# Up projection of the second feed-forward by Strassen's scheme, with the sums of products on VectorE

## The chip, the cores and the metric

The kernel runs on one core of a Trainium2 chip. The metric is the device time of one execution, in microseconds (us); less is better. In the profile PE is TensorE (the matrix engine), PEld its weight loads, DVE VectorE, ACT ScalarE, POOL GpSimd, SP the engine that only issues DMAs.

## What is computed

The reference is one step of a two-layer trunk on 512 latent and 128 context tokens of width 1024. Each layer is a mixer and a gated feed-forward; the change lies in the feed-forward of the second layer:

```python
def conv_ffn(h, w_up, w_conv, w_down):
    a, g = jnp.split(h @ w_up, 2, axis=-1)
    return (jax.nn.gelu(dwconv3(a, w_conv)) * g) @ w_down

xs = xs + gt_s2 * conv_ffn(rmsnorm(xs, g_ffn[l]) * (1.0 + sc_s2) + sh_s2, w_up[l], w_conv_ffn[l], w_down[l])
```

`h` is 640 x 1024, `w_up` 1024 x 5632 (2816 features `a` and 2816 gates `g`), `w_down` 2816 x 1024. `dwconv3` is a convolution of width 3 along the tokens, feature by feature; the context tokens are a sequence of their own. A final RMSNorm follows.

## The kernel before

Features lie on the 128 partitions, the 640 tokens in the free dimension, in two halves of 320 (`HT`); the second half holds 192 latent and 128 context tokens. The 1024 inputs are 8 blocks k of 128, the 2816 features 22 tiles f of 128 (`NF`). Products are in fp32r. So that they are exact enough, each operand is split into a high part (fp32r, cast on ScalarE) and a low part (the rest, a subtraction on VectorE): `XH`, `XL` for the normed tokens, `wh`, `wl` for weights (`split_w`, L94 to L99), `G[:, 0]`, `G[:, 1]` for the hidden layer. A product is the sum of three matmuls, high by high, high by low and low by high, each 128 x 128 by 128 x 320. A tile of 128 outputs and all tokens thus takes 8 x 3 x 2 = 48 matmuls (`mm_k`, L118), where two neighbours, the halves of the tokens, use the same weights.

`ffn` (L373) runs the tiles in the order a_0, g_0, a_1, g_1, ... through `linear` (L125), which loads a tile of weights (512 KB, tag `raw`, four buffers), splits it (tags `wh` and `wl`, three each) and multiplies. Behind an a tile, `conv3` (L348) takes the convolution out of PSUM, once on ScalarE (L350) and four times on VectorE (L353), then comes gelu on ScalarE (L388, tile `ge`). Behind a g tile, VectorE multiplies by the gelu (L398, tile `pr`), ScalarE casts (L400), VectorE subtracts (L401): `G[f]`. The down projection is done in three groups of features (`GROUPS`: 8, 7 and 7), each as soon as its features are there, eight tiles of outputs in a group; `residual` (L328) adds each into `x` with the layer's gate, three VectorE rows. In the last group the last three tiles go half by half (`tail=3`, `mm_half`), so that the final norm of the first half of the tokens (`final_steps`, `rms_steps`, tile `rbfin`) runs while the second is multiplied.

The norm before the feed-forward (`norm_steps`, `norm_part`, L297) runs between the last matmuls of the attention's output projection (`pop`). For each block k VectorE writes the scaled tokens into a small tile `nt`, ScalarE adds the shift and writes `XH`, VectorE subtracts for `XL` (L307). The first three up tiles run half by half with k outermost, so that TensorE can start on the first blocks; their low parts are taken on GpSimd.

A scheduler sets the order on each engine when the program is built; each engine then runs its own list in order, with semaphores between them. PSUM has eight banks of 512 numbers; here three tiles of two banks and two of one (`use_psum(3, 2)`).

## Time and profile before

| | |
|---|---|
| median of three runs | 1732.78 us (1732.56 to 1733.68) |
| span of the profiled execution | 1733.2 us |
| TensorE busy | 1676.1 us, 97% |
| VectorE busy | 1052.3 us, 61% |
| ScalarE busy | 672.4 us, 39% |
| second feed-forward | from about 1250 us to the end |

The profiled execution is given by its span, from the first to the last instruction; it is 0.4 us above the median of the runs. Busy shares are means over stages with different limits. A TensorE row is shown longer than its share of the time, since matmuls overlap: the pace is read from starts.

### The profile page before, as it was taken

The page shows a single profiled execution, that of the slowest core. Times are in us where ns is not written, and L with a number is a line of the kernel's source. Part 1 is how long each engine was busy: PE and PEld are TensorE (multiplying, and loading weights), DVE is VectorE, ACT ScalarE, POOL GpSimd, SP SyncE. Part 2 cuts the span into 40 slices and gives each one's busy share as a digit, 9 for nine tenths or more (in the row PEclk, how much of TensorE's full clock was granted, in tenths as well). Part 3 has the DMA queues.
Part 4 walks back from the last instruction along what each step waited for, and adds up shares of the span by engine and source line. Part 5 has one row for each costly group of instructions (what it writes and reads, how often), then busy time and mean ns, then how long its engine had stood idle before and what let it go on. Part 6 is the DMA issues. An engine that isn't in the chain of part 4 may idle for free. (4 is left out here: it accounts for less than half of the span.)

```text
span 1733.2 us, 28191 instructions
## 1 busy us (share of the span) xinstructions
PE 1676.1 (97%) x11434; PEld 1596.5 (92%) x11434; DVE 1052.3 (61%) x2089; ACT 672.4 (39%) x1235; POOL 142.2 (8%) x150
## 2 busy tenths in 40 slices
PE   5999999999999999999997999999999999999997
PEld 2699889899999999999997888998999999999997
DVE  5886656666987677777376555555564433433444
ACT  6323346754432133223245565555343312321332
POOL 3110001101000000000023212120100000000001
PEclk9999999999999999999999999999999999999998
DMA  8334422141454454453213111211222222222211
GB/s 325 117 132 163 160 72 71 48 142 59 140 176 147 146 153 144 154 170 104 79 64 101 60 60 47 65 42 52 74 73 74 73 74 73 71 76 85 69 54 61
DMA packets 57121, 175.62 MB, mean 101 GB/s; under 512 B 7632, under 2 KB 15104, under 8 KB 56736
## 3 DMA queue, kind: packets, MB, share of 16 engines
q1 hardware_dynamic: 56800, 173.66, 31.1%
q8 instruction: 90, 1.47, 0.4%
...
q0 software_dynamic: 192, 0.17, 0.0%
HBM read 169.61 MB, written 4.20 MB: 100 GB/s over the span
## 5 line engine op out<-in xcount | busy, mean ns | idle before, releaser
L331 DVE SCALAR_TENSOR_TENSOR x<-pd,mod,x 128x320 f32<-128x320 f32 (+2 forms) x144 | 55.1, 434 | 146.7 <-PE pd L122 137.3
L247 DVE CUSTOM_DVE_ANT_0 adj<-adw,cb 128x1024 f32<-128x1024 f32 x112 | 136.7, 1221 | 1.6
L398 DVE TENSOR_TENSOR pr<-pu,ge 128x384 f32<-128x384 f32 x84 | 37.4, 486 | 108.4 <-PE pu L122 107.6
L353 DVE SCALAR_TENSOR_TENSOR fcb<-pu,cwf,fcb 128x384 f32<-128x384 f32 (+1 forms) x176 | 95.8, 549 | 4.1
L388 ACT ACTIVATE ge<-fcb 128x641 f32<-128x641 f32 x44 | 32.6, 742 | 105.4 <-DVE fcb L353 105.4
L306 ACT ACTIVATE XH<-nt,mod 128x192 fp32r<-128x192 f32 (+1 forms) x96 | 39.6, 466 | 44.0 <-DVE nt L302 43.8
L1120 DVE CUSTOM_DVE_ANT_0 s<-pS,bm 128x384 f32<-128x384 f32 x64 | 34.5, 553 | 30.1 <-PE pS L1119 29.0
L307 DVE SCALAR_TENSOR_TENSOR XL<-nt,mod,XH 128x192 fp32r<-128x192 f32 (+1 forms) x96 | 46.4, 521 | 5.0 <-ACT XH L306 4.9
L1021 DVE TENSOR_SCALAR s<-s,nm 128x384 f32<-128x384 f32 (+1 forms) x80 | 46.3, 586 | 1.8
L1019 ACT ACTIVATE s<-s,nm 128x384 f32<-128x384 f32 x64 | 39.2, 612 | 20.3 <-DVE nm L1120 18.3
L350 ACT ACTIVATE fcb<-pu,cwf 128x384 f32<-128x384 f32 x88 | 46.3, 528 | 1.3
L1194 POOL TENSOR_TENSOR fo<-fo,rs 128x320 f32<-128x320 f32 x8 | 6.9, 888 | 469.8 <-ACT rs L1186 469.8
L1134 ACT COPY pTs<-pS 128x384 f32<-128x384 f32 (+1 forms) x80 | 33.7, 434 | 23.4 <-PE pS L1132 22.7
L1132 PE MATMUL pS<-ident,s 128*128 128x128 f32 x208 | 36.3, 281 | 5.8 <-DVE s L1021 5.8
L98 POOL TENSOR_TENSOR qk00l<-qk,qk00h 128x1024 fp32r<-128x1024 f32 x1 | 2.8, 2761 | 461.6 <-DVE rn L288 461.6
L273 ACT ACTIVATE sqn<-x 128x320 f32<-128x320 f32 x56 | 25.3, 466 | 39.4 <-DVE x L331 35.3
L1094 POOL TENSOR_TENSOR bm<-amask,wr 128x768 f32<-128x768 f32 x16 | 30.7, 1918 | 112.6 <-issue 83.9
L302 DVE SCALAR_TENSOR_TENSOR nt<-x,coefA,rbn 128x192 f32<-128x192 f32 (+1 forms) x96 | 36.7, 430 | 3.6 <-PE rbn L294 3.5
L1112 PE MATMUL pS<-k,q 128*128 128x256 f32 x128 | 31.0, 328 | 7.6 <-DVE k L1047 7.1
L400 ACT CAST G<-pr 128x640 fp32r<-128x640 f32 x44 | 31.8, 728 | 13.4 <-DVE pr L398 13.4
L331 DVE SCALAR_TENSOR_TENSOR x<-pop,mod,x 128x320 f32<-128x320 f32 (+2 forms) x36 | 14.4, 433 | 36.7 <-PE pop L122 26.0
L401 DVE TENSOR_TENSOR G<-pr,G 128x640 fp32r<-128x640 f32 x44 | 36.0, 819 | 0.0
...
## 6 DMA issues: line engine op xcount, KB each, us to landing
u<-in_w_up SPq DMA_DIRECT2D x88, 512.0 KB, 3.5
adw<-in_w_adaT SPq DMA_DIRECT2D x56, 512.0 KB, 4.1
wa<-in_w_ada SPq DMA_DIRECT2D x40, 512.0 KB, 5.0
...
qk<-in_w_qkv SPq DMA_DIRECT2D x24, 512.0 KB, 3.5
d<-in_w_down SPq DMA_DIRECT2D x16, 512.0 KB, 3.5
qk<-in_w_ab SPq DMA_DIRECT2D x8, 512.0 KB, 3.5
op<-in_w_oab SPq DMA_DIRECT2D x6, 512.0 KB, 3.4
```

The costliest lines, as they stand in the source:

```text
L247: dve.tensor_tensor_reduce(out=jk, in0=w, in1=cb[:, s], op0=ALU.mult, op1=ALU.add, scale=1.0, scalar=0.0, accum_out=acc[:, k, s : s + 1])
L302: dve.scalar_tensor_tensor(out=t, in0=x[:, k, c0:c1], scalar=coefA[:, n, k, s : s + 1], in1=rb[:, c0 - a * HT : c1 - a * HT], op0=ALU.mult ...
L306: act.activation(out=oh, in_=t, func=AF.Identity, bias=b)
L307: last = dve.scalar_tensor_tensor(out=ol, in0=t, scalar=b, in1=oh.bitcast(F32), op0=ALU.add, op1=ALU.subtract)
L331: r = dve.scalar_tensor_tensor(out=x[:, k, c0:c1], in0=pt[:, h, c0 - h * HT : c1 - h * HT], scalar=mod[:, l, ch, k, s : s + 1], in1=x[:, k ...
L350: act.activation(out=o, in_=i, func=AF.Copy, scale=w[1])
L353: dve.scalar_tensor_tensor(out=o, in0=i, scalar=w[j], in1=o, op0=ALU.mult, op1=ALU.add)
L398: dve.tensor_tensor(out=o, in0=i_, in1=c, op=ALU.mult)
L401: here[0] = dve.tensor_tensor(out=g[:, 1], in0=pr, in1=g[:, 0].bitcast(F32), op=ALU.subtract).ins
L1019: act.activation(out=s, in_=src, func=AF.Exp, scale=-1.0, bias=nm, accum_out=sm)
L1021: dve.tensor_scalar(out=s, in0=s, scalar1=sm, scalar2=None, op0=ALU.mult)
L1132: pe.transpose(pS[:, j * P : (j + 1) * P], s[:, j * P : (j + 1) * P], ident)
```

## The change

The weights of feature tile f are seen as two by two half blocks: a11 and a12 are the a tile's weights for the inputs k = 0 to 3 and 4 to 7, a21 and a22 the g tile's. The tokens are two by two as well: B11 (k 0 to 3, first half of the tokens), B21 (k 4 to 7, first half), B12 and B22 for the second half. The eight half products of a feature are replaced by seven (Strassen's scheme in Winograd's form), from the fourth feature tile on (`NC = 3`), on 19 of 22. With s = a21 + a22 and t = s - a11 the products are: w1 = a11 with B11, w2 = a12 with B21, w3 = a12 - t with B22, w4 = a22 with T4, w5 = s with T1, w6 = t with T2, w7 = a11 - a21 with T3. T1 to T4 are sums of the token blocks, made once (`sums`), T1 in the place of B12. The norm now keeps its scaled tokens in four tiles `keep`, ScalarE adds the shift to them in place (`shift`, 24 rows), VectorE adds and splits them, eight rows of 1280 elements.

Each product is 4 x 3 = 12 matmuls into one bank (`product`). Three banks hold the sums of a feature, partly accumulated by TensorE (A: w1, then w2; B: w6, then w7, then w4; C: w5, then w3), and read in between by ScalarE (`s1`) and VectorE (`u2`, `u3`, `gg`); the convolution then reads SBUF (`av`, tile `fca`). w4 and w3 of a feature come after w1 and w6 of the next. PSUM is eight tiles of one bank from there on. The down projection is done in four groups (6, 6, 5 and 5 features) instead of three. Other lines of the diff move pools, leave out comments, or set `fo` to six buffers.

```diff
+    def ffn_open(es, l):
+        fc = es.enter_context(tc.tile_pool(name=f"fc{l}", bufs=1, reuse_waits="tile"))
+        fp = es.enter_context(tc.tile_pool(name=f"fp{l}", bufs=2, reuse_waits="tile"))
+        def gtile(nm):
+            return fp.tile([P, 2, T], F32R, tag="G", name=nm, bufs=7)
+        keep = [gtile(f"keep{l}{i}").bitcast(F32).rearrange("p a b -> p (a b)").rearrange("p (k c) -> p k c", k=4)
+                for i in range(4)]
+        return fc, fp, gtile, keep
...
+        B11, B21 = ((XH[:, k : k + 4, 0:HT], XL[:, k : k + 4, 0:HT]) for k in (0, 4))
+        T1, B22 = ((XH[:, k : k + 4, HT:T], XL[:, k : k + 4, HT:T]) for k in (0, 4))
+        T2, T3, T4 = ((TT[:, i, 0], TT[:, i, 1]) for i in range(3))
...
+        def split_t(dst, src):
+            act.copy(out=dst[0], in_=src)
+            dve.tensor_tensor(out=dst[1], in0=src, in1=dst[0].bitcast(F32), op=ALU.subtract)
+        def shift(i):
+            a = i // 2
+            for k in range(4):
+                for c0, c1, s in RANGES[a]:
+                    t = keep[i][:, k, c0 - a * HT : c1 - a * HT]
+                    act.activation(out=t, in_=t, func=AF.Identity, bias=mod[:, l, 3, 4 * (i % 2) + k, s : s + 1])
+        def sums():
+            n11, n21, n12, n22 = keep
+            tt = lambda o, a, b, op: dve.tensor_tensor(out=o, in0=a, in1=b, op=op)
+            yield
+            yield
+            shift(2)
+            shift(3)
+            tt(n22, n22, n12, ALU.subtract)
+            split_t(T3, n22)
+            shift(0)
+            yield
+            tt(n12, n12, n11, ALU.subtract)
+            tt(n11, n22, n11, ALU.add)
+            split_t(T2, n11)
+            shift(1)
+            yield
+            tt(n21, n21, n11, ALU.subtract)
+            split_t(T4, n21)
+            yield
+            split_t(T1, n12)
+            yield
+        NC = 3
+        st = sums()
+        linear([I["w_up"][l, i // 2, i % 2] for i in range(2 * NC)], done_up, f"u{l}_", head=3, spare=True,
+               filler=lambda: next(st, 0))
+        use_psum(0, 8)
+        half = [None, 0]
+        def split_half(src, nm):
+            if half[1] == 0:
+                half[0] = [wp.tile([P, 1024], F32R, tag=t, name=f"{nm}{t}") for t in ("wh", "wl")]
+            h, lo = (w[:, 512 * half[1] : 512 * half[1] + 512] for w in half[0])
+            half[1] ^= 1
+            act.copy(out=h, in_=src)
+            dve.tensor_tensor(out=lo, in0=src, in1=h.bitcast(F32), op=ALU.subtract)
+            return h.rearrange("p (k c) -> p k c", c=P), lo.rearrange("p (k c) -> p k c", c=P)
+        def product(pt, w, b, first, last):
+            o = pt[:, :HT]
+            for k in range(4):
+                for n, (ww, xx) in enumerate(((w[0], b[0]), (w[0], b[1]), (w[1], b[0]))):
+                    pe.matmul(o, ww[:, k], xx[:, k], start=(first and k == 0 and n == 0),
+                              stop=(last and k == 3 and n == 2), skip_group_check=not first)
+        def up(f):
+            tt = lambda o, a, b, op: dve.tensor_tensor(out=o, in0=a, in1=b, op=op)
+            ra, rg = (wp.tile([P, 1024], F32, tag="raw", name=f"u{l}_{f}{q}", bufs=4) for q in "ag")
+            sp.dma_start(out=ra, in_=I["w_up"][l, f, 0])
+            sp.dma_start(out=rg, in_=I["w_up"][l, f, 1])
+            a11, a12, a21, a22 = ra[:, 0:512], ra[:, 512:], rg[:, 0:512], rg[:, 512:]
+            A = pst(f"A{l}_{f}")
+            product(A, split_half(a11, f"w1{f}"), B11, True, True)
+            s1 = fp.tile([P, HT], F32, tag="s1", name=f"s1{l}_{f}")
+            act.copy(out=s1, in_=A[:, :HT])
+            yield
+            ss = fp.tile([P, 2, 512], F32, tag="ss", name=f"ss{l}_{f}", bufs=1)
+            tt(ss[:, 0], a21, a22, ALU.add)
+            tt(ss[:, 1], ss[:, 0], a11, ALU.subtract)
+            B = pst(f"B{l}_{f}")
+            product(B, split_half(ss[:, 1], f"w6{f}"), T2, True, True)
+            u2 = fp.tile([P, HT], F32, tag="u2", name=f"u2{l}_{f}")
+            tt(u2, B[:, :HT], s1, ALU.add)
+            yield
+            product(A, split_half(a12, f"w2{f}"), B21, False, True)
+            av = cin.next()
+            act.copy(out=av[:, 1 : HT + 1], in_=A[:, :HT])
+            tt(a12, a12, ss[:, 1], ALU.subtract)
+            yield
+            tt(a21, a11, a21, ALU.subtract)
+            product(B, split_half(a21, f"w7{f}"), T3, False, True)
+            u3 = fp.tile([P, HT], F32, tag="u3", name=f"u3{l}_{f}", bufs=1)
+            tt(u3, B[:, :HT], s1, ALU.add)
+            yield
+            C = pst(f"C{l}_{f}")
+            product(C, split_half(ss[:, 0], f"w5{f}"), T1, True, True)
+            gg = fp.tile([P, T], F32, tag="gg", name=f"gg{l}_{f}")
+            tt(gg[:, HT:], C[:, :HT], u3, ALU.add)
+            yield
+            product(B, split_half(a22, f"w4{f}"), T4, False, True)
+            tt(gg[:, 0:HT], B[:, :HT], s1, ALU.add)
+            yield
+            product(C, split_half(a12, f"w3{f}"), B22, False, True)
+            n = NS - HT
+            tt(av[:, HT + 1 : NS + 1], C[:, 0:n], u2[:, 0:n], ALU.add)
+            tt(av[:, NS + 2 : T + 2], C[:, n:HT], u2[:, n:], ALU.add)
+            c = bufs.next()
+            w = wcols(f)
+            o = c[:, 1 : T + 2]
+            act.activation(out=o, in_=av[:, 1 : T + 2], func=AF.Copy, scale=w[1])
+            for d, j in ((0, 0), (2, 2)):
+                dve.scalar_tensor_tensor(out=o, in0=av[:, d : d + T + 1], scalar=w[j], in1=o, op0=ALU.mult, op1=ALU.add)
+            gelu(f, c)
+            for t, q in tokens(c):
+                tt(gg[:, t], gg[:, t], q, ALU.mult)
+            gate(f, gg)
+            yield
+        SGROUPS = ((0, 6), (6, 12), (12, 17), (17, 22))
+        old = None
+        gi = 0
+        def down(hook=None):
+            nonlocal gi
+            k0, k1 = SGROUPS[gi]
+            linear([I["w_down"][l, o, :, k0:k1] for o in range(KT)], lambda o, pt, a: residual(l, 5, o, pt, a),
+                   f"d{l}_{gi}_", ks=[(k - k0, G[k][:, 0], G[k][:, 1]) for k in range(k0, k1)], nk=k1 - k0, head=0,
+                   tail=3 if k1 == NF else 0, hook=hook)
+            gi += 1
+        for f in range(NC, NF):
+            new = up(f)
+            for who in (0, 1, 0, 1, 0, 0, 0):
+                s_ = new if who == 0 else old
+                if s_ is not None:
+                    next(s_)
+            old = new
+            if gi < len(SGROUPS) - 1 and f == SGROUPS[gi][1]:
+                down()
+        next(old)
+        next(old)
+        et.close()
+        down(mk_hook())
...
-        nrm = es.enter_context(tc.tile_pool(name="nrm2", bufs=2, reuse_waits="tile"))
-        st = norm_steps(1, 1, nrm)
-        out_proj(1, I["w_oc"], range(KT), lambda: next(st))
-        fn = es.enter_context(tc.tile_pool(name="fn", bufs=2, reuse_waits="tile"))
-        fin = final_steps(nrm, fn)
-        ffn(1, list(st)[-1], lambda: next(fin))
+        pools = ffn_open(es, 1)
+        with ExitStack() as en:
+            nrm = en.enter_context(tc.tile_pool(name="nrm2", bufs=2, side="right", reuse_waits="tile"))
+            st = norm_steps(1, 1, nrm, pools[3])
+            out_proj(1, I["w_oc"], range(KT), lambda: next(st))
+            list(st)
+        def mk_hook():
+            nrm = es.enter_context(tc.tile_pool(name="nrm3", bufs=2, side="right", reuse_waits="tile"))
+            fn = es.enter_context(tc.tile_pool(name="fn", bufs=2, side="right", reuse_waits="tile"))
+            fin = final_steps(nrm, fn)
+            return lambda: next(fin)
+        ffn_s(1, pools, mk_hook)
```

VectorE, one feature in the steady up stage, before: `u1_32_7l` and `u1_32_8l` are the low parts of two weight tiles, `fcb` is the convolution's buffer.

```order
L98 TENSOR_TENSOR u1_32_7l_15746<-u1_32_7_15743,u1_32_7h_15745 128x1024
L353 SCALAR_TENSOR_TENSOR fcb10_12430<-pu1_32_4_15562,cwf1_12428,fcb10_12430 128x2x192
L353 SCALAR_TENSOR_TENSOR fcb10_12430<-pu1_32_4_15562,cwf1_12428,fcb10_12430 128x2x128
L353 SCALAR_TENSOR_TENSOR fcb10_12430<-pu1_32_4_15562,cwf1_12428,fcb10_12430 128x2x192
L353 SCALAR_TENSOR_TENSOR fcb10_12430<-pu1_32_4_15562,cwf1_12428,fcb10_12430 128x2x128
L398 TENSOR_TENSOR pr1_18_15674<-pu1_32_5_15625,ge1_18_15617 128x2x192
L398 TENSOR_TENSOR pr1_18_15674<-pu1_32_5_15625,ge1_18_15617 128x2x128
L98 TENSOR_TENSOR u1_32_8l_15807<-u1_32_8_15804,u1_32_8h_15806 128x1024
L401 TENSOR_TENSOR G1_18_15677<-pr1_18_15674,G1_18_15677 128x640
```

VectorE in the up stage of the change, from the middle of one feature to the middle of the next: `u21` and `u31` are `u2` and `u3`, `B1_7` is bank B of feature 7, names that begin with w are halves of weight tiles (a tile holds two products, its name is that of the first), `ss1` holds s and t, `fca` is `av`.

```order
L559 TENSOR_TENSOR u21_7_13784<-B1_7_13767,s11_7_13747 128x320
L559 TENSOR_TENSOR ss1_8_13903<-ss1_8_13903,u1_8a_13865 128x512
L559 TENSOR_TENSOR u1_8g_13866<-u1_8a_13865,u1_8g_13866 128x512
L559 TENSOR_TENSOR fca11_12413<-C1_6_13333,u21_6_13269 128x192
L559 TENSOR_TENSOR fca11_12413<-C1_6_13333,u21_6_13269 128x128
L547 TENSOR_TENSOR w47wl_13887<-u1_7g_13727,w47wh_13886 128x512
L547 TENSOR_TENSOR w47wl_13887<-ss1_8_13903,w47wh_13886 128x512
L604 SCALAR_TENSOR_TENSOR fcb10_12420<-fca11_12413,cwf1_12410,fcb10_12420 128x641 x2
L559 TENSOR_TENSOR u31_7_13844<-B1_7_13767,s11_7_13747 128x320
L547 TENSOR_TENSOR w37wl_13924<-u1_7a_13726,w37wh_13923 128x512
L547 TENSOR_TENSOR w37wl_13924<-u1_8a_13865,w37wh_13923 128x512
L559 TENSOR_TENSOR gg1_6_13348<-gg1_6_13348,fcb10_12420 128x512
```

Nine rows a feature have become 22, and rows that read PSUM (`u21`, `fca`, `u31`) stand between the low parts that later products wait for; the other ten rows of the period are of the same kinds.

TensorE, an up tile before: each row is a pair of matmuls on the same weights.

```order
L122 MATMUL pu1_18_6_14402<-XH_68,u1_18_6h_14398 128x320 x2
L122 MATMUL pu1_18_6_14402<-XL_69,u1_18_6h_14398 128x320 x2
L122 MATMUL pu1_18_6_14402<-XH_68,u1_18_6l_14399 128x320 x2
L122 MATMUL pu1_18_6_14402<-XH_68,u1_18_6h_14398 128x320 x2
L122 MATMUL pu1_18_6_14402<-XL_69,u1_18_6h_14398 128x320 x2
L122 MATMUL pu1_18_6_14402<-XH_68,u1_18_6l_14399 128x320 x2
```

TensorE now, where product w2 of feature 7 ends (bank A) and w7 begins (bank B, which VectorE's `u21` row above reads first):

```order
L554 MATMUL A1_7_13730<-XH_68,w27wh_13811 128x320
L554 MATMUL A1_7_13730<-XL_69,w27wh_13811 128x320
L554 MATMUL A1_7_13730<-XH_68,w27wl_13812 128x320
L554 MATMUL B1_7_13767<-TT1_12409,w27wh_13811 128x320 x2
L554 MATMUL B1_7_13767<-TT1_12409,w27wl_13812 128x320
```

Before, a block of weights stood for two or four matmuls in succession (the halves of the tokens, and high and low tokens with high weights); now for two with high weights and one with low ones. The order of w7 is the same as that of w2 (the pair in its row is T3's high and low part). The program still issues one weight load for each matmul.

VectorE at the opening, before: the last row of the norm, then the low parts of up tiles 3 and 4 and the convolution of tile 0.

```order
L307 SCALAR_TENSOR_TENSOR XL_69<-nt37_512_12418,mod_71,XH_68 128x128
L98 TENSOR_TENSOR u1_0_3l_12632<-u1_0_3_12629,u1_0_3h_12631 128x1024
L98 TENSOR_TENSOR u1_0_4l_12695<-u1_0_4_12692,u1_0_4h_12694 128x1024
L353 SCALAR_TENSOR_TENSOR fcb10_12430<-pu1_0_0_12460,cwf1_12428,fcb10_12430 128x2x192
L98 TENSOR_TENSOR u1_0_5l_12758<-u1_0_5_12755,u1_0_5h_12757 128x1024
L353 SCALAR_TENSOR_TENSOR fcb10_12430<-pu1_0_0_12460,cwf1_12428,fcb10_12430 128x2x128
```

The same place now, from the row behind the norm's last one on (`keep10` to `keep13` are the four kept token blocks, `TT1` holds T2 to T4):

```order
L512 TENSOR_TENSOR keep13_11775<-keep13_11775,keep12_11774 128x1280
L103 TENSOR_TENSOR u1_3l_12639<-u1_3_12636,u1_3h_12638 128x1024
L512 TENSOR_TENSOR keep12_11774<-keep12_11774,keep10_11772 128x1280
L361 SCALAR_TENSOR_TENSOR fcb10_12420<-pu1_0_12446,cwf1_12410,fcb10_12420 128x2x192
L500 TENSOR_TENSOR TT1_12409<-keep13_11775,TT1_12409 128x1280
L361 SCALAR_TENSOR_TENSOR fcb10_12420<-pu1_0_12446,cwf1_12410,fcb10_12420 128x2x128
L361 SCALAR_TENSOR_TENSOR fcb11_12421<-pu1_2_12448,cwf1_12410,fcb11_12421 128x2x192
L361 SCALAR_TENSOR_TENSOR fcb10_12420<-pu1_0_12446,cwf1_12410,fcb10_12420 128x2x192
L361 SCALAR_TENSOR_TENSOR fcb11_12421<-pu1_2_12448,cwf1_12410,fcb11_12421 128x2x128
L361 SCALAR_TENSOR_TENSOR fcb10_12420<-pu1_0_12446,cwf1_12410,fcb10_12420 128x2x128
L361 SCALAR_TENSOR_TENSOR fcb11_12421<-pu1_2_12448,cwf1_12410,fcb11_12421 128x2x192
L512 TENSOR_TENSOR keep10_11772<-keep13_11775,keep10_11772 128x1280
```

u_3's low part now stands behind one sum of 1280 elements. u_4's comes four rows behind these (one of the convolution and the product with the gate, two rows, lie between): it stands behind three sums, a low part of 1280 elements, eight rows of the convolution and that product.

## Rows read from the trace of the kernel before

**Rows 1.** The page: the span, and busy time (share of the span) of each engine

```profile
span 1733.2 us, 28191 instructions
...
PE 1676.1 (97%) x11434; PEld 1596.5 (92%) x11434; DVE 1052.3 (61%) x2089; ACT 672.4 (39%) x1235; POOL 142.2 (8%) x150
```

**Rows 2.** Stretches of 100 us: length, each engine's busy us (instructions), granted clock, DMA share, GB/s

```profile
1500.00:1600.00 100.00, 100.00 (x684) 100.00 (x683) 40.85 (x68) 24.16 (x31) 0.00 (x0) 1.00 0.24 75
...
1700.00:1733.00 33.00, 20.80 (x140) 20.23 (x139) 16.22 (x43) 10.15 (x22) 6.87 (x8) 0.83 0.23 80
```

**Rows 3.** What TensorE waits for from 1200 us on: us in total, times, longest

```profile
PE rbfin L294 <- DVE dgfin L291: 2.7, 1, 2.7
...
PE pop L122 <- DVE x L331: 1.5, 1, 1.5
...
PE pu L113 <- DVE x L331: 0.4, 1, 0.4
```

**Rows 4.** TensorE in order of time, one up tile: start, length, line, count

```profile
1660.50 0.46 PE L122 MATMUL pu<-XH,u_11h 128*128 128x320 f32 x2
...
1667.54 0.75 PE L122 MATMUL pd<-G,d_0h 128*128 128x320 f32 x4
```

**Rows 5.** TensorE in order of time, the first matmuls of the last three down tiles

```profile
1698.34 0.31 PE L113 MATMUL pd<-G,d_5h 128*128 128x320 f32 x1
...
1698.78 0.31 PE L113 MATMUL pd<-G,d_5h 128*128 128x320 f32 x1
```

**Rows 6.** VectorE in order of time, up stage: start, length, count [idle before]

```profile
1457.33 1.23 DVE L98 TENSOR_TENSOR u_5l<-u,u_5h 128x1024 fp32r<-128x1024 f32 x1 [5.00 <-ACT u_5h L97]
1458.48 2.31 DVE L353 SCALAR_TENSOR_TENSOR fcb<-pu,cwf,fcb 128x384 f32<-128x384 f32 x4
...
1464.46 1.22 DVE L98 TENSOR_TENSOR u_6l<-u,u_6h 128x1024 fp32r<-128x1024 f32 x1
1465.59 0.82 DVE L401 TENSOR_TENSOR G<-pr,G 128x640 fp32r<-128x640 f32 x1
```

**Rows 7.** VectorE in order of time, at the second norm

```profile
1254.32 0.54 DVE L302 SCALAR_TENSOR_TENSOR nt<-x,coefA,rbn 128x320 f32<-128x320 f32 x1
1254.78 0.48 DVE L274 TENSOR_TENSOR accn<-accn,sqn 128x320 f32<-128x320 f32 x1
1255.18 0.54 DVE L302 SCALAR_TENSOR_TENSOR nt<-x,coefA,rbn 128x320 f32<-128x320 f32 x1
```

**Rows 8.** VectorE in order of time, down stage

```profile
1400.23 1.14 DVE L331 SCALAR_TENSOR_TENSOR x<-pd,mod,x 128x320 f32<-128x320 f32 x3 [4.77 <-PE pd L122]
1401.28 1.22 DVE L98 TENSOR_TENSOR d_5l<-d,d_5h 128x1024 fp32r<-128x1024 f32 x1
```

**Rows 9.** ScalarE in order of time, up stage

```profile
1456.25 1.05 ACT L97 CAST u_5h<-u 128x1024 fp32r<-128x1024 f32 x1 [5.02 <-PE pu L122]
```

**Rows 10.** The page's DMA issues: count, KB each, median us from issue to landing

```profile
u<-in_w_up SPq DMA_DIRECT2D x88, 512.0 KB, 3.5
```

**Rows 11.** VectorE in order of time, end of the second norm

```profile
1270.14 0.35 DVE L307 SCALAR_TENSOR_TENSOR XL<-nt,mod,XH 128x128 fp32r<-128x128 f32 x1 [0.47 <-ACT XH L306]
1272.44 1.23 DVE L98 TENSOR_TENSOR u_3l<-u,u_3h 128x1024 fp32r<-128x1024 f32 x1 [1.95 <-ACT u_3h L97]
```

**Rows 12.** TensorE in order of time, start of up tile 3

```profile
1273.31 0.46 PE L122 MATMUL pu<-XH,u_3h 128*128 128x320 f32 x2
```

**Rows 13.** ScalarE in order of time, second half of the second norm

```profile
1260.46 1.10 ACT L306 ACTIVATE XH<-nt,mod 128x192 fp32r<-128x192 f32 x3 [3.76 <-DVE nt L302]
1262.31 1.07 ACT L306 ACTIVATE XH<-nt,mod 128x128 fp32r<-128x128 f32 x3 [0.74 <-DVE nt L302]
```

**Rows 14.** VectorE in order of time, last residual of the first half

```profile
1707.78 0.55 DVE L331 SCALAR_TENSOR_TENSOR x<-pd,mod,x 128x320 f32<-128x320 f32 x1 [1.44 <-PE pd L116]
```

**Rows 15.** TensorE in order of time, end of the last down stage

```profile
1717.34 0.31 PE L116 MATMUL pd<-G,d_7l 128*128 128x320 f32 x1
1717.49 0.38 PE L294 MATMUL rbfin<-dgfin,ones 128*128 128x128 f32 x2
```

More of the change, by code (lines that the diff above doesn't have):

```diff
@@ L60, in pst, with pm2 @@
         return psum["s"].tile([P, 512], F32, tag="ps", name=nm)
+    def pm2(nm):
+        return pmt(nm) if psum["shape"][0] else tuple(pst(f"{nm}_{a}") for a in range(2))
     def bank(pt, a):
@@ L142, in linear @@
             else:
-                pts = [pmt(f"p{nm}{i + j}") for j in range(g)]
+                pts = [pm2(f"p{nm}{i + j}") for j in range(g)]
             if g == 1:
@@ L295, in rms_steps, with norm_part @@
         yield pb
-    def norm_part(l, which, nrm, a, rb, ks):
+    def norm_part(l, which, nrm, a, rb, ks, keep=None):
         n = 2 * l + which
@@ L309, in norm_part, with norm_steps @@
         return last.ins
-    def norm_steps(l, which, nrm):
+    def norm_steps(l, which, nrm, keep=None):
         n = 2 * l + which
@@ L319, in norm_steps @@
         yield
-        norm_part(l, which, nrm, 0, rb, range(0, 6))
+        norm_part(l, which, nrm, 0, rb, range(0, 6), keep)
         yield
@@ L323, in norm_steps @@
         rb1 = next(s1)
-        norm_part(l, which, nrm, 0, rb, range(6, KT))
+        norm_part(l, which, nrm, 0, rb, range(6, KT), keep)
         yield
-        yield norm_part(l, which, nrm, 1, rb1, range(KT))
+        yield norm_part(l, which, nrm, 1, rb1, range(KT), keep)
     def residual(l, ch, k, pt, a=None):
@@ L330, in residual @@
             for c0, c1, s in RANGES[h]:
-                r = dve.scalar_tensor_tensor(out=x[:, k, c0:c1], in0=pt[:, h, c0 - h * HT : c1 - h * HT],
+                r = dve.scalar_tensor_tensor(out=x[:, k, c0:c1], in0=bank(pt, h)[:, c0 - h * HT : c1 - h * HT],
                                              scalar=mod[:, l, ch, k, s : s + 1], in1=x[:, k, c0:c1],
@@ new lines, in ffn_s, with gate, gelu, wcols @@
+    def ffn_s(l, pools, mk_hook):
+        fc, fp, gtile, keep = pools
+        et = ExitStack()
+        tp = et.enter_context(tc.tile_pool(name=f"tp{l}", bufs=1, side="right", reuse_waits="tile"))
+        TT = tp.tile([P, 3, 2, 4, HT], F32R, name=f"TT{l}")
+        cw = fc.tile([P, NF, 3], F32, name=f"cwf{l}")
+        sp.dma_start(out=cw, in_=I["w_conv_ffn"][l])
+        cin = ConvBufs(fc, 2, f"fca{l}")
+        bufs = ConvBufs(fc, 2, f"fcb{l}")
+        G = [None] * NF
+        ge = {}
+        B11, B21 = ((XH[:, k : k + 4, 0:HT], XL[:, k : k + 4, 0:HT]) for k in (0, 4))
+        T1, B22 = ((XH[:, k : k + 4, HT:T], XL[:, k : k + 4, HT:T]) for k in (0, 4))
+        T2, T3, T4 = ((TT[:, i, 0], TT[:, i, 1]) for i in range(3))
+        def gate(f, pr):
+            g = G[f] = gtile(f"G{l}_{f}")
+            act.copy(out=g[:, 0], in_=pr)
+            dve.tensor_tensor(out=g[:, 1], in0=pr, in1=g[:, 0].bitcast(F32), op=ALU.subtract)
+        def gelu(f, c):
+            ge[f] = c
+            act.activation(out=c[:, 1 : T + 2], in_=c[:, 1 : T + 2], func=AF.Gelu_apprx_tanh)
+        def wcols(f):
+            return [cw[:, f, j : j + 1] for j in range(3)]
+        def done_up(i, pt, _):
+            f = i // 2
+            if i % 2 == 0:
+                gelu(f, conv3(bufs.next(), pt, wcols(f)))
+                return
+            pr = fp.tile([P, T], F32, tag="gg", name=f"gg{l}_{f}")
+            c = ge[f]
+            if isinstance(pt, tuple):
+                for a, q, n, c1 in ((0, 0, HT, 1), (1, 0, NS - HT, HT + 1), (1, NS - HT, T - P0, NS + 2)):
+                    t0 = a * HT + q
+                    dve.tensor_tensor(out=pr[:, t0 : t0 + n], in0=pt[a][:, q : q + n], in1=c[:, c1 : c1 + n], op=ALU.mult)
+            else:
+                for o, i_, c_ in zip(halves(v2(pr)), halves(pt), conv_parts(c, 1)):
+                    dve.tensor_tensor(out=o, in0=i_, in1=c_, op=ALU.mult)
+            gate(f, pr)
+        def split_t(dst, src):
[123 more added lines that the diff above has]
+        down(mk_hook())
@@ L1188, in apply @@
             for kq in range(4):
[L1189 removed]
+                o = fn.tile([P, 2, HT], F32, tag="fo", name=f"fo{a}{kq}", bufs=6)
                 for k in range(2):
```

9 lines of the change are left out of this document (6 added, 3 removed).

## The prediction

> **What bounds the kernel now.** I read the page first: TensorE is busy 97% of a 1733.2 us span, VectorE 61%, ScalarE 39% [rows 1]. Then the stretches of 100 us of the second feed-forward: TensorE starts 684 matmuls in each, VectorE is busy about 40 of 100 us, the granted clock is 1.00 [rows 2]. Then the list of what TensorE waits for from 1200 us on: six waits, 8.5 us together, at the second norm (pop, rbn, pu) and in the final norm (rbfin), none between [rows 3]. So from 1255 to 1717 us the time is the number of matmuls times their pace. The pace comes from one up tile: its 48 matmuls start at 1660.50 us, the next tile's at 1667.54: 7.04/48 = 0.1467 us, 14.08 us for a feature (two tiles) [rows 4]. The page counts a weight load for every matmul [rows 1]. In those rows a block of weights stands for two or four matmuls in succession, in the new products for one or two, as in the last down tiles; there three matmuls take 0.44 us, 0.147 each [rows 5]. The price of a matmul is the same in both forms.
>
> **What goes.** Seven products of 12 matmuls stand for 96: 84 a feature, on 19 features, 228 fewer (before 10740 in the program, now 10512). 228 x 0.1467 = 33.4 us, if TensorE stays the bound. A feature would then last 12.32 us.
>
> **What comes, in the steady stage.** VectorE does 22 instructions a feature instead of 9. By length: 11 of 512 in SBUF (seven low halves of weights, four weight sums), 640 (G), 512 and 128 (the product with the gate), two of 641 (the convolution), and out of PSUM four of 320, one of 192, one of 128. That is 9794 elements. From starts that follow at once: 1024 elements 1.13 us (u_6l, then G) [rows 6], 320 in SBUF 0.40 (accn), 320 with PSUM 0.46 (nt) [rows 7]; so 1.042 ns an element, and 0.065 us a row in SBUF, 0.127 with PSUM. 9794 elements are 10.2 us, 16 x 0.065 + 6 x 0.127 = 1.8, and the second convolution row must wait for the first to end, 0.15: 12.15 us of VectorE against 12.32 of TensorE. It fits by 1%. The upper bound takes each row's whole duration, since nearly all of them stand behind a wait: 640 elements 0.82 us, 1024 1.22 us, 0.153 above the elements' time [rows 6]: 10.2 + 22 x 0.153 = 13.6 us. I take 12.15: the starts of [rows 6] are also rows behind waits (u_6l waits for ScalarE), and start while the row ahead is still shown as busy.
>
> [...]
>
> Why a tie costs little: VectorE need not be in step. TensorE's order is w1(f), w4(f-1), w6(f), w3(f-1), w2(f), w7(f), w5(f). The tightest return is bank B: w7 may start when u2 has been read from it after w6, and between them stand w3 and w2, 24 matmuls, 3.5 us; u3 has as much (w5 and w1) before w4. In the order of VectorE the weights stand ahead of these reads. So VectorE may lag about 3 us before TensorE stops, and after every five or six features a down stage sets the lag to zero: 8 tiles of 36 matmuls, 5.3 us, in each of which VectorE has a split of 768 elements, 0.87 us, and a residual of three rows, 1.05 us [rows 8]. Up to 12.8 us a feature is then free (0.5 x 6 = 3). I put 1 us for the stage.
>
> ScalarE gets 7 casts of half length, two PSUM copies of 320, one convolution row, gelu and cast: with 1.05 us for 1024 [rows 9] some 7.5 of 12.3 us. Its hand-over to VectorE is short (cast ends 1457.30, u_5l starts 1457.33) [rows 6, 9]. SP issues 8 more down loads of fewer bytes each. A raw tile is now held until w3 of the next feature is split; its next user comes some 6 us later, a load lands in 3.5 us [rows 10]. The 8 further residuals lie in the down stages. I price all this at nothing; if a load came late, it would be 1 to 2 us a feature.
>
> **The opening.** Here cover is thin. Before, the last low part of the norm ends at 1270.5 us, tile 3 starts on TensorE at 1273.31 and wants u_3l at 1273.9; u_3l ends at 1273.67 [rows 11, 12]. Now VectorE has, behind the norm, n22-n12 (1280 elements: 1.40 us), u_3l 1.14, n12-n11 1.40, the low part of T3 1.40, n11+n22 1.40, eight convolution rows (two times 2.31 from [rows 6], some 4.0 as two chains alternate), gg_0 0.81, and then u_4l 1.14: 12.7, with the last shift on ScalarE (0.40, a third of the XH rows' 1.10 and a little more [rows 13]) 13.1 us. So u_4l ends at 1283.6. TensorE, which now begins tiles 4 and 5 with 8 matmuls ahead of it, wants it at 1273.3 + 7.04 + 1.17 = 1281.5. Stall 2.1 us. By the same walk u_5l is just in time, the first Strassen product waits about 0.3 us for the convolution of tile 4 (its bank), and the first w7 about 0.8 us for u2. In the norm itself ScalarE gets 24 shifts of 0.35 to 0.55 us between its XH rows; in the second half those rows fill 1.1 of each 1.85 us [rows 13], and a shift each doubles that to 2.2: 16 of them may delay the norm by up to 2.5 us; half of it reaches TensorE, 1.5 us with the first half. Opening: 4.7, taken as 5; bounds 0, and 9 with whole durations in the walk and the norm's whole delay on TensorE.
>
> **The ends.** After the last up product the chain is av, convolution on ScalarE and VectorE, gelu, product, cast, low part: about 7 us, under 40 matmuls of the last down stage, 5.9 us: 1 us. The last stage has 5 instead of 7 features, so the final pass over the second half has 45 matmuls instead of 63, 2.6 us less. The first half's final norm lies under it: from its last residual at 1707.78 to its rbfin at 1717.49, which comes at once behind TensorE's last down matmul [rows 14, 15]. It is covered to the microsecond, so I charge 2 us; bounds 0 and 2.6.
>
> **Sum.** 1733.2 - 33.4 + 5 + 1 + 1 + 2 = 1708.8 us of span. The page gives the profiled execution by its span, which is 0.4 us above the median of the runs, 1732.78: 1708.4, say 1709.
>
> **Rivals.**
> 1. VectorE pays whole durations and becomes the bound, the other side. 13.6 us, plus 0.4 for in-order waits on TensorE and ScalarE (a row waits until its product ends), is 14.0: 19 x 0.08 = 1.5 us gained, 9 lost: 1740. It decides at 13.6 us a feature (19 x 0.48 = 9). For it: nearly every new row waits for another engine or for the row ahead. Against it: [rows 6, 7]. Chance 0.11. [...]
> 2. VectorE sets part of the pace: 12.9 to 13.5 us, because some rows overlap and some don't, or because slots of weights (three tiles, two halves each) come free late and each cast stands bare before its low part. 13.2 gives 19 x 0.88 = 16.7 gained, 8 lost: 1724; the span of it 1714 to 1729. Chance 0.25.
> 3. It comes out even, between these two: 0.04.
> 4. TensorE's pace falls, by its loads or by its clock. The loads: [rows 5] show the same 0.147 us. The clock is 1.00 here; gaps of a microsecond at the norm left it there, and it is lower (0.83) only in the last 33 us, with 20.8 busy [rows 2]. No chance of its own; it would lift rivals 1 and 2.
>
> **How the numbers follow.** Forecast, TensorE-bound with small losses: 0.60, 1702 to 1714 by the bounds above (33.4 us less 3 to 15 us of losses, where the sum has 9). With rival 2 the range that leaves out two in ten runs from 1702 to 1727. Changes within 0.2% (3.5 us) can hardly be told from none here. Faster: forecast 0.60, rival 2 0.25: 0.85. Within 0.2%: 0.04. Slower: 0.11.
>
> **What the profile would show.** In a stretch between two down stages: about 68 matmuls in 10 us, VectorE busy 95% or more, ScalarE 60%. If right, waits of TensorE there sum to under 3 us and VectorE's rows of 512 start 0.60 us apart. If rival 1, they start 0.69 apart, and TensorE waits at w7 and w4 (bank B) for u2 and u3 on VectorE in every feature. The opening is right if tile 4 waits 1 to 4 us for u_4l. The end is right if rbfin of the first half comes 1 to 3 us behind the last down matmul. What would make it wrong: VectorE above 12.8 us a feature, or a raw tile that lands late.

## The result, and the profile after

The changed kernel takes 1705.47 us (median of 4 runs, 1704.28 to 1707.02); the kernel before, on the same chips, 1733.16. The ratio is 0.9838, 95% interval 0.9824 to 0.9852: 27.7 us faster. The forecast was 1709, range 1702 to 1727.

The page of the changed kernel, with the lines that answer to [rows 1]:

```profile
span 1705.2 us, 28246 instructions
...
PE 1644.9 (96%) x11206; PEld 1563.0 (92%) x11206; DVE 1188.9 (70%) x2376; ACT 732.4 (43%) x1385; POOL 141.8 (8%) x153
```

Two stretches, columns as in [rows 2]: 100 us with both stages in it, and four features between two down stages:

```profile
1500.00:1600.00 100.00, 100.00 (x684) 100.00 (x683) 75.84 (x143) 40.58 (x69) 0.00 (x0) 1.00 0.27 80
1391.90:1441.70 49.80, 49.80 (x341) 49.80 (x340) 48.79 (x91) 27.55 (x48) 0.00 (x0) 1.00 0.29 85
```

TensorE starts 684 matmuls in 100 us, as before. Between two down stages VectorE is busy 98% and ScalarE 55%, and TensorE still never stops.

What TensorE waits for from 1270 us on (total, times, longest), beside [rows 3]:

```profile
PE rbfin L299 <- DVE dgfin L296: 4.2, 2, 3.5
PE pu L127 <- DVE u_4l L103: 1.0, 1, 1.0
PE rbfin L283 <- DVE accfin L279: 0.8, 1, 0.8
PE pu L127 <- DVE fcb L361: 0.8, 1, 0.8
PE A L554 <- ACT s L567: 0.6, 1, 0.6
```

The waits for u_4l, fcb and s are in the opening and at the first Strassen feature; from 1304 to 1658 us there is no wait in the list. Beside [rows 11, 12], VectorE in the opening, in order of time:

```profile
1270.79 0.35 DVE L315 SCALAR_TENSOR_TENSOR XL<-keep,mod,XH 128x128 fp32r<-128x128 f32 x1 [0.60 <-ACT XH L314]
1271.61 1.49 DVE L512 TENSOR_TENSOR keep<-keep,keep 128x1280 f32<-128x1280 f32 x1 [0.47 <-ACT keep L508]
1273.02 1.22 DVE L103 TENSOR_TENSOR u_3l<-u,u_3h 128x1024 fp32r<-128x1024 f32 x1
...
1280.40 1.48 DVE L512 TENSOR_TENSOR keep<-keep,keep 128x1280 f32<-128x1280 f32 x1
1281.80 0.48 DVE L361 SCALAR_TENSOR_TENSOR fcb<-pu,cwf,fcb 128x256 f32<-128x256 f32 x1
1282.19 0.88 DVE L495 TENSOR_TENSOR gg<-pu,fcb 128x384 f32<-128x384 f32 x2
1282.99 1.21 DVE L103 TENSOR_TENSOR u_4l<-u,u_4h 128x1024 fp32r<-128x1024 f32 x1
```

and TensorE, which waits for the last convolution row (a bank for tile 5) and for u_4l:

```profile
1281.14 0.46 PE L127 MATMUL pu<-XL,u_4h 128*128 128x320 f32 x2
1282.42 0.53 PE L127 MATMUL pu<-XH,u_5h 128*128 128x320 f32 x2 [0.83 <-DVE fcb L361]
1282.79 0.45 PE L127 MATMUL pu<-XL,u_5h 128*128 128x320 f32 x2
1284.26 0.56 PE L127 MATMUL pu<-XH,u_4l 128*128 128x320 f32 x2 [1.01 <-DVE u_4l L103]
...
1301.59 0.41 PE L554 MATMUL A<-XH,w23wh 128*128 128x320 f32 x1 [0.56 <-ACT s L567]
```

u_4l ends at 1284.20; the forecast's walk had 1283.6. The last wait is for `s1`, which ScalarE copies out of bank A; the copy stands behind a cast that waits for VectorE's sum u_3g (ScalarE, in order of time):

```profile
1300.59 0.62 ACT L546 CAST w23wh<-u_3g 128x512 fp32r<-128x512 f32 x1 [0.47 <-DVE u_3g L559]
1301.11 0.42 ACT L567 COPY s<-A 128x320 f32<-128x320 f32 x1
```

The end, TensorE beside [rows 15]:

```profile
1688.31 0.31 PE L121 MATMUL pd<-G,d_7l 128*128 128x320 f32 x1
1689.33 0.94 PE L299 MATMUL rbfin<-dgfin,ones 128*128 128x128 f32 x6 [0.71 <-DVE dgfin L296]
1691.10 0.80 PE L283 MATMUL rbfin<-ones,accfin 128*128 128x1 f32 x6 [0.83 <-DVE accfin L279]
1695.40 1.65 PE L299 MATMUL rbfin<-dgfin,ones 128*128 128x128 f32 x6 [3.51 <-DVE dgfin L296]
```

**Where the 28.0 us between the two spans come from.** I lay the two traces side by side at two marks: the start of up tile 3 and the last down matmul (d_7l).

| | before | after |
|---|---|---|
| start to tile 3 | 1273.31 | 1273.55 |
| tile 3 to last down matmul | 444.03 | 414.76 |
| last down matmul to the end | 15.86 | 16.89 |

The middle stretch lost 228 x 0.1467 = 33.4 us and got 4.1 us of gaps between starts that follow later than the pace: 3.8 in the opening, 0.3 at the last G, 0.1 at the final norm. When the changed kernel runs a second time (below) this stretch repeats to 0.03 us, while over all the runs the start of tile 3 lies anywhere from 1269.3 to 1273.6 us with the same code ahead of it. Effects of a microsecond are therefore read from the stretch and not from the whole time. A run's time stands 1.8 us above its span (1707.02 with 1705.2).

### The profile page after: what moved, and what is told of

It is laid out like the page before. It is cut to its first block, busy times and chain, and to the rows that moved or that the text cites. A ratio compares the mean times of both kernels' runs of the same rounds, so it can differ in the third digit from the quotient of the medians.

```text
span 1705.2 us, 28246 instructions
## 1 busy us (share of the span) xinstructions
PE 1644.9 (96%) x11206; PEld 1563.0 (92%) x11206; DVE 1188.9 (70%) x2376; ACT 732.4 (43%) x1385; POOL 141.8 (8%) x153
## 5 line engine op out<-in xcount | busy, mean ns | idle before, releaser
L339 DVE SCALAR_TENSOR_TENSOR x<-pd,mod,x 128x320 f32<-128x320 f32 (+2 forms) x168 | 64.1, 434 | 126.4 <-PE pd L127 120.5
L361 DVE SCALAR_TENSOR_TENSOR fcb<-pu,cwf,fcb 128x384 f32<-128x384 f32 (+1 forms) x100 | 53.9, 547 | 1.9
L406 DVE TENSOR_TENSOR pr<-pu,ge 128x384 f32<-128x384 f32 (+1 forms) x42 | 18.7, 485 | 50.1 <-PE pu L127 49.2
L314 ACT ACTIVATE XH<-nt,mod 128x192 fp32r<-128x192 f32 (+1 forms) x72 | 29.7, 467 | 35.7 <-DVE nt L310 35.6
L396 ACT ACTIVATE ge<-fcb 128x641 f32<-128x641 f32 x22 | 16.3, 742 | 52.0 <-DVE fcb L361 52.0
L315 DVE SCALAR_TENSOR_TENSOR XL<-nt,mod,XH 128x192 fp32r<-128x192 f32 (+1 forms) x72 | 35.0, 523 | 4.2 <-ACT XH L314 4.2
L604 DVE SCALAR_TENSOR_TENSOR fcb<-fca,cwf,fcb 128x641 f32<-128x641 f32 x38 | 33.5, 883 | 3.5 <-ACT fcb L602 3.2
L1336 PEld LDWEIGHTS pS<-ident,s 128*128 128x128 f32 x208 | 23.6, 141 | 11.6 <-DVE s L1225 9.8
L279 DVE TENSOR_TENSOR accn<-accn,sqn 128x320 f32<-128x320 f32 x56 | 28.9, 522 | 7.2 <-ACT sqn L278 6.2
L127 PE MATMUL pd<-G,d_0h 128*128 128x320 f32 x176 | 33.2, 309 | 0.0
```

The source lines that it names most:

```text
L127: pe.matmul(bank(pt, a)[:, : sp_[a][1] - sp_[a][0]], ww[:, kt], xx[:, slice(*sp_[a])], start=(first and n == 0), stop=(last and n == 2))
L315: last = dve.scalar_tensor_tensor(out=ol, in0=t, scalar=b, in1=oh.bitcast(F32), op0=ALU.add, op1=ALU.subtract)
L339: r = dve.scalar_tensor_tensor(out=x[:, k, c0:c1], in0=bank(pt, h)[:, c0 - h * HT : c1 - h * HT], scalar=mod[:, l, ch, k, s : s + 1], in1= ...
L361: dve.scalar_tensor_tensor(out=o, in0=i, scalar=w[j], in1=o, op0=ALU.mult, op1=ALU.add)
L1336: pe.transpose(pS[:, j * P : (j + 1) * P], s[:, j * P : (j + 1) * P], ident)
```

## The experiments

"The theory" is the prediction's: TensorE sets the pace, VectorE's rows cost their distance from start to start, and VectorE may lag about 3 us.

**One and two rows more of VectorE a feature.** Where is the edge?

```diff
             tt(ss[:, 1], ss[:, 0], a11, ALU.subtract)
+            tt(ss[:, 1], ss[:, 0], a11, ALU.subtract)
```

> One more VectorE row of 512 elements a feature (the weight sum for w6 is worked out twice, the result is the same). By starts 0.60 us apart a feature costs VectorE 12.75 us against 12.32 of TensorE, 0.43 more a feature. Theory (a lag of about 3 us is free and each down stage sets it to zero): at most 6 x 0.43 = 2.6 us of lag in a group, so hardly a wait between 1310 and 1655 us; 1 to 3 us in the opening and at the last G; 1707.5 us. Rival A (no slack: all that VectorE is longer than TensorE is lost): 19 x 0.43 = 8.2 us, 1713.7. Rival B (VectorE pays whole durations, 0.68 a row, and sets the pace already): 12.9 us, 1718.

> Two more VectorE rows of 512 a feature (the same sum three times in all): 13.35 us against 12.32, 1.03 more a feature. Theory: 3 us of lag are free in each group but the first, which begins late from the opening: 4.1 + (6.2 - 3) + (5.2 - 3) + (4.1 - 3) = 10.6, and 1 at the last G: 1717 us, the waits at w7 and w4 for u2 and u3. Rival A: 19 x 1.03 = 19.6, 1725. Rival B: 19 x 1.36 = 25.8, 1731. If TensorE does not wait at all, the cost of a VectorE row is far less than its pitch here.

One row: 1704.07 us, ratio 0.9831 (0.9817 to 0.9845); the stretch is 415.0 us, 0.25 more than without. It is free, where 1707.5 was expected. Two rows: 1713.66, ratio 0.9885 (0.9871 to 0.9898); the stretch is 423.4, 8.7 more, where the theory had 11.6. What TensorE waits for there from 1270 to 1660 us:

```profile
PE C L554 <- DVE w621wl L547: 1.5, 1, 1.5
PE C L554 <- DVE w611wl L547: 1.5, 1, 1.5
PE C L554 <- DVE w617wl L547: 1.5, 1, 1.5
PE B L554 <- ACT w13wh L546: 1.4, 1, 1.4
PE pu L127 <- DVE u_4l L103: 1.0, 1, 1.0
PE pu L127 <- DVE fcb L361: 0.8, 1, 0.8
```

Once in each of the last three groups, late in it (during features 11, 17 and 21), TensorE's next start comes 1.65 us later than its pace of 0.1467 us (1.49 of that is the wait). That is 5 us, where full loss (rival A) asks 1.03 us in every feature and whole durations (rival B) more still. The first group paid 1.4 us at its first w6, and 1.5 us went in a stretch with a granted clock of 0.57 (last section).

The lag itself can be read from the traces. For each low half of weights, take the time from the end of its VectorE row to the start of the first matmul that reads it. This is the least of these leads (us) in each sixth of the up stage between the first and the second down stage, about one feature:

| | 1 | 2 | 3 | 4 | 5 | 6 |
|---|---|---|---|---|---|---|
| changed kernel | 5.55 | 5.47 | 5.16 | 5.11 | 5.16 | 5.11 |
| one row more | 5.54 | 5.02 | 3.83 | 3.50 | 1.85 | 1.62 |
| two rows more | 5.55 | 3.39 | 1.86 | 0.25 | 0.06 | 0.18 |

Behind the next down stage it begins at 5.55 again in all three; behind the third it dips at the first w6 (3.71, 2.02 and 0.21) and is at 5.5 or more again for w7. So lag builds up unseen, shows only when the lead is used up, and a down stage clears it, as the theory has it; the edge is between one row and two. The leads fall faster than the added rows explain: with one row more VectorE needs 12.5 us against TensorE's 12.32, 0.2 a feature, and the lead falls by 0.8. The scheduler orders VectorE's rows anew when rows are added; how much of the fall is order stays open.

The place was another than I had forecast: not bank B (u2, u3), but the low half of w3, which shares its slot with w6 (the slot bears the name of w6) and stands behind the rows put in. It is also not the same order of matmuls. With two rows the scheduler put w3 of the feature before ahead of w6 at all three stops (TensorE, in order of time):

```profile
1438.58 0.31 PE L554 MATMUL C<-XH,w611wh 128*128 128x320 f32 x1
...
1440.53 0.41 PE L554 MATMUL C<-XH,w611wl 128*128 128x320 f32 x1 [1.49 <-DVE w611wl L547]
1440.78 0.46 PE L554 MATMUL B<-TT,w611wh 128*128 128x320 f32 x2
```

In the changed kernel, and with one row more, the 12 matmuls of w6 come first, and TensorE's order is the same in both. Where and how long TensorE stops with two rows is therefore an effect of lag and of this order together; the run doesn't tell them apart.

**Putting off the sums in the opening.**

```diff
             shift(0)
             yield
+            yield
             tt(n12, n12, n11, ALU.subtract)
...
             shift(1)
-            yield
             tt(n21, n21, n11, ALU.subtract)
```

> In the opening the sums of the kept blocks behind the first step are taken up one tile later, so that u_4l stands ahead of two sums of 1280 and eight convolution rows on VectorE. Theory (each sum has 9 to 26 us until its product, only u_4l and the banks of tile 5 are wanted at once): the waits of 0.83 and 1.01 us at tiles 4 and 5 go, 1.5 to 2.2 us with what stands around them: 1703.5. Rival: VectorE is busy without a break from 1271.6 to 1310 us, so the wait only moves to the first products (s1, u2): no change, 1705.5.

1706.58 us, ratio 0.9846 (0.9833 to 0.986); the stretch is 416.2, 1.4 more. The waits at tile 4 are gone, and in their place stands

```profile
PE pu L127 <- DVE u_5l L103: 2.6, 1, 2.6
```

after which the granted clock was 0.50 from 1292 to 1295 us, where pairs of matmuls started 0.53 us apart instead of 0.29. My expectation was wrong: VectorE has no free time here, and what was put off stood in front of the next low part. The rival was right that the wait only moves, though it moved to u_5l and not to the first products. By starts behind the pace the new wait takes 2.9 us where the two at tile 4 took 2.3, and 0.6 us less is lost at the first Strassen feature; the 1.4 us more are those of the stretch with the clock at 0.50.

**The same rows on an engine that is free.** `pooled` names the tiles of the plain part whose low part GpSimd makes.

```diff
-               filler=lambda: next(st, 0))
+               filler=lambda: next(st, 0), pooled=(4, 5))
```

> Low parts of up tiles 4 and 5 (u_4l, u_5l) on GpSimd, which has no work from 1255 us to the last 30 us; VectorE has two rows of 1.13 us less in the opening. A row of 1024 took GpSimd 2.5 us on tiles 0 to 2 of this stage, so u_4l would be there at about 1277, u_5l at about 1280, before tile 4 begins. Theory: the wait for u_4l (1.2 us with what stands around it) goes, the one at tile 5 for the convolution (1.0) and the one for s1 (0.8) stay or shrink, since VectorE is 2.3 us ahead from then on: from tile 3 to the last down matmul 412 to 413.5 us instead of 414.8, in all 1703.5. Rival: VectorE is late by more than those two rows, the wait returns at the first products: 414.8. Second rival: GpSimd's rows slow VectorE's beside them: worse than 414.8.

> The same, and the sums behind the first step taken up one tile later, as in the run before that only delayed them. There u_5l came too late (2.6 us); here it is on GpSimd, so this wait cannot come. Theory: no wait of more than 0.5 us from tile 3 to the first product: 411.5 to 412.5 us from tile 3 to the last down matmul, 1702.5. Rival: what was put off is late at T2 for w6 or at the low part of w1: a wait of 1 to 3 us at the first products, 413 to 415.

1701.99 us, ratio 0.9824 (0.9811 to 0.9838), stretch 413.6, 1.2 less, just above the 412 to 413.5 expected: the wait for u_4l is gone, one of 0.6 for the convolution is left, and one of 0.5 for a low part of w6 stands where that for s1 was. Behind the last down matmul it is 17.3 us, 0.4 more than in the changed kernel, because dgfin comes later; the cause of that is open.

With the sums put off as well: 1704.01, stretch 413.55, so the 411.5 to 412.5 expected did not come. From tile 3 on the order on every engine is that of the run without the second edit, and the waits are the same; the second edit tells nothing, and the 2 us between the two times are spread between runs.

Beside VectorE's rows GpSimd took longer than 2.5 us for a row (GpSimd, in order of time):

```profile
1270.01 3.63 POOL L103 TENSOR_TENSOR u_4l<-u,u_4h 128x1024 fp32r<-128x1024 f32 x1 [21.19 <-ACT u_4h L102]
1273.60 3.65 POOL L103 TENSOR_TENSOR u_5l<-u,u_5h 128x1024 fp32r<-128x1024 f32 x1
```

and a VectorE row of 1280 beside them twice as long as in the changed kernel (1.49), so that two rows of 1.13 us gave back less than their time; the second rival is right in part:

```profile
1271.95 3.03 DVE L500 TENSOR_TENSOR TT<-keep,TT 128x1280 fp32r<-128x1280 f32 x1
```

**The weight sums on GpSimd.** Would VectorE's work cost TensorE something that no wait shows, taking it away would help.

```diff
-            tt(ss[:, 0], a21, a22, ALU.add)
+            pp(ss[:, 0], a21, a22, ALU.add)       # pp: pool.tensor_tensor
...
-            tt(a21, a11, a21, ALU.subtract)
+            pp(a21, a11, a21, ALU.subtract)
```

> The four weight sums of each feature on GpSimd instead of VectorE. VectorE then needs 12.15 - 4 x 0.60 = 9.75 us a feature, GpSimd about 4 x 1.3 = 5.2. Theory (TensorE sets the pace between 1304 and 1658 us, VectorE only keeps up): no gain in the steady stage, up to 1 us in the opening: 1704.5 to 1705.5 us. Rival A (VectorE still costs TensorE something that no wait shows): 2 to 4 us faster. Rival B (a GpSimd row holds up VectorE for its time): 9.75 + 5.2 = 14.95 us of VectorE a feature, waits in every feature, up to 19 x 2.6 - 10 = 40 us slower.

1707.0 us, ratio 0.9848 (0.9834 to 0.9861), stretch 416.9, 2.2 more. The first Strassen product loses 1.5 us, since it waits for a convolution row, but the 1.1 us lost behind it in the changed kernel are gone, so the opening is only 0.4 us longer; the other 1.8 us are lost in the steady stage, in pieces under 0.5. No gain, as the theory has it, and even a small loss. Rival A is not tested to the end, because VectorE is still busy 246.9 of the 340 us from 1310 to 1650 us (262.1 in the changed kernel). Rival B is partly right: some rows of either engine are longer beside the other's, 1.49 us instead of 0.68 on VectorE and 1.75 instead of 1.28 on GpSimd (rows below). GpSimd's sums also come later: the least lead of the low parts falls to 3.4 us, where the changed kernel keeps 5.1. GpSimd, in order of time:

```profile
1311.98 1.30 POOL L570 TENSOR_TENSOR ss<-ss,u_5a 128x512 f32<-128x512 f32 x1
1313.24 1.75 POOL L570 TENSOR_TENSOR u_5g<-u_5a,u_5g 128x512 f32<-128x512 f32 x1
```

and VectorE beside it:

```profile
1311.83 0.49 DVE L559 TENSOR_TENSOR u<-B,s 128x320 f32<-128x320 f32 x1 [0.95 <-PE B L554]
1312.33 1.49 DVE L547 TENSOR_TENSOR w15wl<-u_5a,w15wh 128x512 fp32r<-128x512 f32 x1
1313.75 1.78 DVE L547 TENSOR_TENSOR w15wl<-u_4g,w15wh 128x512 fp32r<-128x512 f32 x1
1315.45 0.54 DVE L559 TENSOR_TENSOR fca<-C,u 128x192 f32<-128x192 f32 x2
```

A low part that lasts 0.68 alone lasts 1.49: it ends at 1313.82, 0.54 behind GpSimd's row (1313.28). The next GpSimd row in turn ends 1.75 behind its start instead of 1.28, and the VectorE row beside that one (1.78) ends at 1315.53, again 0.54 behind it. The row that reads bank B (0.49) beside the first GpSimd row is not longer: its mean in the changed kernel is 0.48. Moving the rows gave back only part of their time here: from 1310 to 1650 us VectorE has 72 rows fewer, 43 us at 0.60 from start to start, and is busy 15.3 us less.

**Without the shift.**

```diff
                     t = keep[i][:, k, c0 - a * HT : c1 - a * HT]
-                    act.activation(out=t, in_=t, func=AF.Identity, bias=...)
```

> Leaves out the 24 ScalarE rows that add the shift to the kept token blocks (so the products T2 to T4 miss it). The prediction charged 1.5 us of TensorE for these rows in the norm. Theory from the trace: they lie in ScalarE's idle time and cost TensorE nothing in the norm; only the first sum starts 0.5 us sooner, so tile 4 waits 0 to 0.5 us less: 414.3 to 414.8 us from tile 3 to the last down matmul, and the distance from the second norm's last rbn to tile 3 unchanged. Rival (the charge was right, hidden elsewhere): that distance is 1 to 1.5 us shorter.

One run: the stretch is 414.3, 0.5 less, since the first sum starts 0.8 us sooner. From the rbn of the second half of the tokens to tile 3 it is 14.15 us, with the shift 14.17, before the change 14.16; from the rbn of the first half 28.71, 28.35 and 28.70. The shift rows cost TensorE nothing in the norm.

**Seven features in the last down group, and both gains together.**

```diff
-        SGROUPS = ((0, 6), (6, 12), (12, 17), (17, 22))
+        SGROUPS = ((0, 5), (5, 10), (10, 15), (15, 22))
```

> Down projection in groups of 5, 5, 5 and 7 features instead of 6, 6, 5 and 5, so that the final pass over the second half of the tokens has 63 matmuls again. Theory (the 45 matmuls are too little cover for the first half's final norm): the 1.0 us between the last down matmul and the first half's rbfin goes, 1704.5. Rival: the end is set by the final norm of the second half alone, whose chain is as long as before: no change, 1705.5, with rbfin just as far ahead of it.

> Both edits that gained by themselves: u_4l and u_5l on GpSimd, and down groups of 5, 5, 5 and 7. They lie 380 us apart, so they should add: from tile 3 to the last down matmul 413.6 + 0.2 = 413.8 us, behind it 16.2 to 16.6 us instead of 16.9; beside the changed kernel, which is run again here on the same chip, 1.5 us less. Rival: the second does nothing for the time (its gain is within the spread): 1.0 us less.

> The changed kernel itself once more, on the chip of the other two, to compare with: 1705 us, from tile 3 to the last down matmul 414.8 us and behind it 16.9 us, as in its first profile, if those stretches repeat as they did in the other runs.

Seven features: 1704.23 us, ratio 0.9833 (0.9819 to 0.9846), which the spread of the runs cannot tell from the changed kernel. The stretches can: 16.2 us behind the last down matmul instead of 16.9, 0.2 more ahead of it (TensorE, at the end):

```profile
1686.16 0.31 PE L121 MATMUL pd<-G,d_7l 128*128 128x320 f32 x1
1686.31 0.83 PE L299 MATMUL rbfin<-dgfin,ones 128*128 128x128 f32 x6
```

rbfin comes at once again. With u_4l and u_5l on GpSimd as well: stretch 413.8, tail 16.2, 1702.68 us, ratio 0.9829 (0.9815 to 0.9844). The changed kernel beside it, on the same chip: 414.7, 16.9, 1703.99 us, ratio 0.9833 (0.982 to 0.9847). So the two add, 1.7 us by the stretches (1.0 ahead of the last down matmul, 0.7 behind it) and 1.3 by the medians; the intervals of the ratios overlap, and only the stretches show it.

**Strassen one feature later.** With this edit feature 3's plain tiles read T1, which the last sum writes over the first four channel blocks of the second half of the tokens; the trace shows no wait of TensorE for it.

```diff
-        NC = 3
+        NC = 4
```

> Strassen from the 5th feature tile on instead of the 4th: feature 3 in the plain form, 12 matmuls more. Theory (a feature gains 12 x 0.1467 us, and the waits of the opening at tiles 4 and 5 come from the sums, not from the first Strassen feature): 1.76 us more, less 0 to 1 us of the waits at the first products: 415.5 to 416.5 us from tile 3 to the last down matmul, 1706.5. Rival (the waits come from the first Strassen features on top of the sums, so that a later start gives back more than it costs): 411 to 414 us.

1706.46 us, ratio 0.985 (0.9835 to 0.9864), stretch 418.25, 3.5 more: 1.76 for the 12 matmuls, 1.5 in the opening, where from 1281.1 to 1284.3 us pairs of matmuls start 0.53 us apart instead of 0.29, as with two rows more, and 0.2. The waits at tiles 4 and 5 are the same to 0.01 us, so they do not come from the first Strassen features. The forecast of 415.5 to 416.5 missed by that stretch, and by a wait of 1.1 us at the first Strassen product in place of those that went.

## Why the prediction was right, step by step

- **What goes**: right. 228 matmuls less between the two marks, 33.4 us at the same 0.1467 us each; the rival that TensorE's pace falls by its loads is out.
- **The steady stage**: right, and better than charged: 0 us instead of 1. VectorE's starts (in order of time, between two down stages):

```profile
1426.12 0.68 DVE L559 TENSOR_TENSOR u_10a<-u_10a,ss 128x512 f32<-128x512 f32 x1
1426.72 0.68 DVE L547 TENSOR_TENSOR w710wl<-u_10g,w710wh 128x512 fp32r<-128x512 f32 x1
1427.33 0.48 DVE L559 TENSOR_TENSOR gg<-B,s 128x320 f32<-128x320 f32 x1
1427.73 0.68 DVE L547 TENSOR_TENSOR w710wl<-ss,w710wh 128x512 fp32r<-128x512 f32 x1
```

 Rows of 512 start 0.60 us apart while one is shown with 0.68, also where the next row reads what another engine wrote (w710wl a cast of ScalarE, gg bank B). Rows of 320 with PSUM take 0.40, where the forecast had 0.46. Summed over the 22 rows this is 11.9 us a feature (forecast 12.15), so rivals 1 and 2 fall. That VectorE may lag, and that a down stage clears the lag, is shown by the leads above. The 3 us of the forecast were worked out for bank B, and they are not measured: in the up stage of the table the rows that read bank B end at least 2.2 us ahead of the next product into it, and with one row more at least 2.0. What runs out with two rows more is the lead of the low parts, 5.5 us behind a down stage, which the forecast had not named as the tight place.
- **ScalarE, loads, residuals at nothing**: right. ScalarE is busy 55% (forecast 60), and no load stands in the list of waits.
- **The opening**: the walk was right for VectorE up to u_4l (1284.20 for 1283.6), and TensorE at tile 4 loses 2.3 us in two pieces for 2.1; the first piece, the bank for tile 5, was not in it. Behind that the sum is near and the places are not: 0.9 is lost for s1, through ScalarE, and 0.25 at the first w7 for u2, where 0.3 for the convolution and 0.8 for u2 stood; 0.3 at tile 3 for u_3l was not in it. The step that failed in size is the shift in the norm: 1.5 charged, 0 measured. I had doubled ScalarE's rows and let half of the delay through; ScalarE had the room. What the shift costs lies on VectorE behind the norm: without it the last row of the norm comes 0.4 us sooner against the rbn ahead of it, the first sum 0.8 us sooner, and the stretch is 0.5 us shorter. Of 5 us, 3.8 were lost.
- **The ends**: 0.3 instead of 1 at the last G, and 1.0 instead of 2 behind the last down matmul; the cause of the second (45 matmuls for 63) is shown by the run with seven features.
- **The sum**: losses of 9 us were forecast; measured are 3.8 + 0.3 + 0.1 + 1.0 + 0.2 (start of tile 3) = 5.4. The last 0.2 is no loss of the change, since that start differs by 4 us between runs. All the 3.6 us that the forecast was too slow are charges that were too high, those of the opening and of the end inside their bounds. VectorE's narrow fit was not luck: one row more is still free.
